# The gates' activation by tanh, one projection at a time and written over the projection's sum, in a fused attention and gating kernel

## The chip, the cores and the metric

The kernel runs on one core of a Trainium2 chip. The metric is the device time of one execution in microseconds; the median of several runs counts. Before the change it is 807.99 us (three runs: 807.52, 807.99 and 809.23).

Five engines work side by side, each through its own queue of instructions in order: TensorE (PE) multiplies matrices into the accumulators of PSUM, VectorE (DVE) and ScalarE (ACT) work on elements, GpSimd (POOL) does a few selections and issues DMAs, SyncE (SP) issues most DMAs.

## The reference

One layer of a trunk on 512 tokens of width 2048: a norm, attention over a sliding window of 128 keys with 32 heads of 64 (4 heads of keys and values), a gate on the attention's output, an output projection, and a second gate that adds an embedding. Cut to what matters here:

```python
hn = rmsnorm(x, norm_g)
q, k, v, gate = split(hn @ w_in)                 # gate: 512 x 2048
...
out = einsum('bnhgqj,bnjhd->bnqhgd', probs, vb)  # attention, 512 x 2048
y = (out * jax.nn.silu(gate)) @ w_out            # silu(x) = x * sigmoid(x)
x = x + y
x = x + (p @ ple_proj) * sigmoid(rmsnorm(x, ple_norm) @ ple_gate)
return rmsnorm(x, final_g)
```

The change concerns `out * silu(gate)` alone.

## The kernel before

All large products are made of three matmuls each (lines 120 to 122): every operand is split into a high part `hi`, a rounded copy made by ACT, and a low part `lo`, the difference made by DVE. Weights come by DMA as raw tiles of 128 x 1024; ACT makes `whi` (line 106) and DVE `wlo` (line 107), in pools of three buffers, two tiles ahead of their use.

The work has four parts, one after another on PE.

1. The start: keys, values and the first two tiles of queries, out of the first part of the weights.
2. The attention stage, from about 73 to 461 us. Thirty projection units, fourteen of queries (`qps`) and sixteen of gates (`gps`, gate c = 0 to 15, a pair of heads each), of 48 matmuls of 128 x 512 each, are dealt out in small portions between 64 attention blocks. Block i gives the scores of four heads and 64 queries (line 376), which DVE and ACT turn into probabilities (lines 385 to 408: bias, maximum, exponential, sum, scaling). Two blocks later `turn` transposes them on PE (418) and splits the result into `r`: a copy by ACT (420) and a difference by DVE (421). In three blocks of four POOL then selects a part into `own` (430) and ACT copies a half of it (437). One block after that `weigh` multiplies with the values on PE (454, and 456 with `own`), and ACT and DVE gather the result into `U` (463, 464).
3. The output projection, seven products of half matrices per side (`ORDER_OUT`), whose left operands are forms of the gated values (sums and differences of quarters, line 651, split by 658, 659, 663 and 664) and whose weights come as pieces `braw`, split into `bhi` (558) and `blo` (559).
4. The second gate with its embedding, in the same manner, and the final norm and stores.

PE, SP and POOL take the attention stage's instructions in the order in which the code gives them. ACT and DVE are ordered by the scheduler, which places each instruction when its inputs are due; on the chip each engine then keeps to its order and waits where an input is late.

The gates: when the last matmul of a gate's unit is done, DVE multiplies the sum in PSUM with the norm's factor `rb` into one of the four tiles `gates[g]` of 128 x 4 x 512 (line 688), and this frees the PSUM bank (tag "p", two banks). When the four gates of a tile are there, `silu` runs one ACT instruction over the whole tile (line 483); for the last tile three gates together and then one. From then on the gates are open. As soon as also the values of their heads are weighed, `gate_value` multiplies gate and `U` on DVE (line 478), one gate at a time.

A function of ACT stands in a table that a load instruction brings in (ACT_TABLE_LOAD in the profile). The exponential of the attention and the Silu use different tables here, so the program has loads at lines 405 and 483.

Of the kernel before, what the change touches and what calls it, by code (L numbers as in the profile page):

```python
# [13 lines left out]
AF = mybir.ActivationFunctionType  # L14
ALU = mybir.AluOpType
# [38 lines left out]
def trunk_kernel(ctx: ExitStack, tc: tile.TileContext, a: dict):  # L54
    nc = tc.nc
# [22 lines left out]
    def quarter(name):  # L78
        return whole.tile([P, 4, S], F32, tag="quarter", name=name)

    def bank(name, tag):
        return others.get(tag, psum).tile([P, 512], F32, tag=tag, name=name)
# [34 lines left out]
    def mm3(ps, sh, sl, mh, ml, first, last, more=False):  # L117


        nc.tensor.matmul(ps, sh, mh, start=first, stop=False, skip_group_check=more)  # L120
        nc.tensor.matmul(ps, sh, ml, start=False, stop=False, skip_group_check=more)  # L121
        nc.tensor.matmul(ps, sl, mh, start=False, stop=last, skip_group_check=more)  # L122
# [47 lines left out]
    kinds, g = [], 0  # L170
# [11 lines left out]
    rb = kvq.tile([P, S], F32, name="rb")  # L182
# [3 lines left out]
    for k in range(KC):  # L186
# [13 lines left out]
        if k == 0:  # L200
# [3 lines left out]
            out=l, in0=xr, scalar=g1, in1=h.bitcast(F32), op0=ALU.mult, op1=ALU.subtract  # L204
# [15 lines left out]
        for t in range(2):  # L220
            c = slice(t * P, (t + 1) * P)
            mm3(kt_ps[t], wh[:, c], wl[:, c], h, l, f, e)
        for t in range(NB):
            c = slice(t * P, (t + 1) * P)
# [30 lines left out]
    def evac_q(c, ps):  # L255

        q = Q[c] = kvq.tile([P, UNITS, 2, HB], F32R, tag="q", name=f"q{c}", bufs=4)
        halves = slice(0, 64), slice(64, 128)
        for e in range(2):
            src = ps[halves[e]].rearrange("p (g q) -> p g q", q=HB)  # L260
            hi, lo = q[halves[e], :, e], q[halves[1 - e], :, e]
            nc.scalar.copy(hi, src)
            nc.vector.tensor_sub(lo, src, hi.bitcast(F32))
# [58 lines left out]
    U, T, PT, O, gates, biases = {}, {}, {}, {}, {}, {}  # L322
# [148 lines left out]
    weighed, open_gates, due = set(), set(), []  # L471
    ah, al = {}, {}

    def gate_value():

        c = due.pop(0)
        src = gates[c // 4][:, c % 4, :]
        nc.vector.tensor_mul(src, src, U[c // 2][:, c % 2])

    def silu(g, some):  # L480

        part = gates[g][:, some]
        nc.scalar.activation(part, part, AF.Silu)
        for c in range(4 * g + some.start, 4 * g + some.stop):
            open_gates.add(c)
            if c in weighed:
                due.append(c)

# [20 lines left out]
    def block(nm, r, c, jj, m):  # L511
        return a[nm][2 * (c - 1) + jj, 4 * (r - 1) + m]
# [158 lines left out]
    def projections():  # L671
        for m, (kind, c) in enumerate(kinds):
            ps = bank(f"{kind}ps{c}", "p")
            for k in range(KC):
                if m == len(kinds) - 1 and k % 8 == 0:
                    B.ahead(k // 8 - 2)
                if m == len(kinds) - 1 and 2 <= k:
                    next(first_form, None)
                wh, wl = W.get(2 * m + k // 8)
                mm3(ps, wh[:, k % 8, :], wl[:, k % 8, :], xh[k], xl[k], k == 0, k == KC - 1)  # L680
                if k == KC - 1:
                    if kind == "q":
                        evac_q(c, ps)
                    else:
                        g = c // 4
                        if c % 4 == 0:
                            gates[g] = quarter(f"gate{g}")
                        nc.vector.tensor_mul(gates[g][:, c % 4, :], ps, rb)
                        if g == 3 and c % 4 >= 2:
                            silu(g, slice(0, 3) if c % 4 == 2 else slice(3, 4))  # L690
                        elif c % 4 == 3:
                            silu(g, slice(0, 4))
                yield

    proj = projections()

    during = ExitStack()
# [9 lines left out]
    for i in range(blocks + 3):  # L707

        if 2 <= i < blocks + 2:
            turn(i - 2)  # L710
        if 3 <= i:
            weigh(i - 3)
        if i < blocks:
            scores(i)
            first_chores(i)
            if i in (6, 20, 36):
                make_key(1 + i // 16)
        todo = left // (blocks + 2 - i) if i < blocks + 2 else 0
        left -= todo
        for n in range(todo):  # L720
            if n == 5 and due:
                gate_value()
            next(proj)
        if i < blocks:
            for n in range(i * SUM_STEPS // blocks, (i + 1) * SUM_STEPS // blocks):
                sum_weights(n)
    for _ in proj:
        pass
    while due:
        gate_value()  # L730
# [32 lines left out]
    def unit(p, jj, at, forms, todo):  # L763

        ps = banks(p, jj, forms.nm)
        f = forms.made[p]
        first = p not in (6, 5, 3)
        for m in range(4):
            bh, bl = B.get(at[p, jj] + m)
            for kk in range(2):  # L770
                k = 2 * m + kk
                fh, fl = f[m]
                for tb in range(2):
                    mm3(ps[tb], fh[:, kk, blk(tb)], fl[:, kk, blk(tb)], bh[kk], bl[kk], first and k == 0, k == 7, not first)
            some_later(4 - m)
            todo()
        return ps
# [52 lines left out]
    for n, p in enumerate(ORDER_OUT):  # L830
        nxt = out_forms.steps(ORDER_OUT[n + 1]) if n < 6 else iter(())
        for jj in range(2):
# [15 lines left out]
            ps = unit(p, jj, at_out, out_forms, todo)  # L848
# [101 lines left out]
    for n, p in enumerate(ORDER_PLE[:-1]):  # L950
        nxt = ple_forms.steps(ORDER_PLE[n + 1])
        for jj in range(2):
# [16 lines left out]
            ps = unit(p, jj, at_ple, ple_forms, todo)  # L969
# [51 lines left out]
    g = block(0, 0, "s", "o")()  # L1021
# [10 lines left out]
    g = block(1, 0, "s", "t")()  # L1032
# [10 lines left out]
    g = block(0, 1, "p", "o")()  # L1043
# [12 lines left out]
    g = block(1, 1, "p", "t", slice(0, 256))()  # L1056
# [74 lines left out]
```

## Time and profile before

| what | before |
|---|---|
| median of three runs | 807.99 us |
| the profiled execution, its own time | 807.1 us |
| its span in the profile | 805.1 us |
| ACT, table loads at lines 405 and 483 | 8 x 1.283 us |
| ACT, Silu (line 483) | 3 x 1.916, 1.492 and 0.631 us |
| DVE, gate times `rb` (line 688) | 16 x 0.686 us |
| DVE, gate times value (line 478) | 16 x 0.682 us |

A line of the timeline gives the start in us from the span's start, the duration, the engine, the line of the kernel, the operation, what it writes and reads, and in brackets the idle time of the engine before it and what ended this. A line of the groups gives the count, the busy time in us and the mean ns of one, then the idle time before them. A line of the waits gives who waited for whom: us in total, times, the longest.

### The profile page before, as it was taken

The numbers are of one execution on the slowest core, as the hardware profiler recorded it, in microseconds if no ns is written. First come the engines' busy times: TensorE is split into PE (matmuls) and PEld (weight loads), VectorE is DVE, ScalarE is ACT, GpSimd is POOL, SyncE is SP. The second block draws the span as 40 slices with busy tenths as digits, with TensorE's granted clock in tenths as the row PEclk, the third lists the DMA queues.
The fourth block names the chain that finished last, engine by engine and source line by source line (L and its number), as shares of the span: only waits on it lengthen the run. The fifth ranks groups of instructions, "written<-read, shape, count | busy, mean of one in ns | idle before, by whom it ended". The sixth has DMA issues, their size and how long they took to land.

```text
span 805.1 us, 11083 instructions
## 1 busy us (share of the span) xinstructions
PE 792.3 (98%) x3828; PEld 664.8 (83%) x3828; DVE 583.4 (72%) x951; ACT 508.4 (63%) x1034; POOL 111.1 (14%) x216
## 2 busy tenths in 40 slices
PE   9999999999999999999999999999999999999995
PEld 8888888878888888888888888888888888878884
DVE  4547676777767787776777898766646977889685
ACT  5644466676667786666586754555568856758545
POOL 0102113122121313122121100030000020210000
PEclk9999999999999999999999999999999999999998
DMA  8762687768697877877685469898512996895533
GB/s 330 288 196 89 170 277 196 222 186 212 163 255 216 192 235 187 219 184 220 180 211 142 118 215 359 326 283 240 198 53 85 368 204 208 168 212 193 183 105 105
DMA packets 45144, 164.91 MB, mean 205 GB/s; under 512 B 5904, under 2 KB 8080, under 8 KB 41248
## 3 DMA queue, kind: packets, MB, share of 16 engines
q1 hardware_dynamic: 38080, 130.07, 47.5%
q0 software_dynamic: 6720, 33.61, 22.6%
q8 instruction: 30, 0.49, 0.2%
q10 hardware_dynamic: 288, 0.52, 0.2%
q14 instruction: 26, 0.21, 0.1%
HBM read 158.36 MB, written 46.19 MB: 254 GB/s over the span
## 4 chain that ended last, share of the span: by engine, by line
PE 86%; issue 8%; DVE 2%; POOL 1%; DMA 1%; ACT 0%; ACTq 0%; POOLq 0%; DVEq 0%
PE qps L122 7%; PE qps L121 7%; PE qps L120 7%; PE gps L121 7%; PE gps L122 7%; PE gps L120 7%; PE o L122 6%; PE o L121 6%; PE o L120 6%; PE s L376 2%; PE g L121 2%; PE g L122 2%; PE g L120 2%; PE o L454 2%; PE pt L418 2%
## 5 line engine op out<-in xcount | busy, mean ns | idle before, releaser
L559 DVE TENSOR_TENSOR blo<-braw,bhi 128x1024 fp32r<-128x1024 f32 x80 | 97.8, 1222 | 39.9 <-ACT bhi L558 39.7
L558 ACT CAST bhi<-braw 128x1024 fp32r<-128x1024 f32 x80 | 84.0, 1050 | 56.9 <-PE o L122 17.5
L122 PE MATMUL gps<-xh,wlo 128*128 128x512 f32 x256 | 100.2, 391 | 0.0
L121 PE MATMUL gps<-xl,whi 128*128 128x512 f32 x256 | 100.2, 391 | 0.0
L120 PE MATMUL gps<-xh,whi 128*128 128x512 f32 x256 | 99.9, 390 | 0.0
L107 DVE TENSOR_TENSOR wlo<-wraw,whi 128x1024 fp32r<-128x1024 f32 x60 | 73.3, 1222 | 23.8 <-ACT whi L106 20.7
L122 PE MATMUL qps<-xh,wlo 128*128 128x512 f32 x224 | 87.8, 392 | 0.0
L121 PE MATMUL qps<-xl,whi 128*128 128x512 f32 x224 | 87.7, 391 | 0.0
L120 PE MATMUL o<-bhi,fho 128*128 128x512 f32 x224 | 87.7, 391 | 0.0
L122 PE MATMUL o<-bhi,flo 128*128 128x512 f32 x224 | 87.2, 389 | 0.0
L121 PE MATMUL o<-blo,fho 128*128 128x512 f32 x224 | 87.2, 389 | 0.0
L120 PE MATMUL qps<-xh,whi 128*128 128x512 f32 x224 | 87.2, 389 | 0.0
L106 ACT CAST whi<-wraw 128x1024 fp32r<-128x1024 f32 x60 | 62.9, 1049 | 27.9 <-PE gps L121 13.3
L405 ACT ACTIVATE t<-t,sm 128x129 f32<-128x129 f32 x128 | 50.6, 397 | 45.1 <-DVE sm L402 45.1
L121 PE MATMUL g<-blo,fhg 128*128 128x512 f32 x192 | 74.9, 390 | 0.4 <-DVE blo L559 0.4
L120 PE MATMUL g<-bhi,fhg 128*128 128x512 f32 x192 | 75.1, 391 | 0.0
L122 PE MATMUL g<-bhi,flg 128*128 128x512 f32 x192 | 74.8, 390 | 0.0
L430 POOL TENSOR_SCALAR_AFFINE_SELECT own<-r 64x512 fp32r<-64x512 f32 (+1 forms) x48 | 33.1, 690 | 298.4 <-DVE r L421 293.6
L122 PEld LDWEIGHTS gps<-xh,wlo 128*128 128x128 f32 x256 | 48.0, 188 | 10.2
L120 PEld LDWEIGHTS gps<-xh,whi 128*128 128x128 f32 x256 | 48.1, 188 | 9.0
L121 PEld LDWEIGHTS gps<-xl,whi 128*128 128x128 f32 x256 | 48.1, 188 | 8.9
L559 DVE TENSOR_TENSOR blo<-grown,bhi 128x1024 fp32r<-128x1024 f32 x32 | 39.1, 1222 | 17.4 <-ACT bhi L558 17.4
(202 smaller groups left out, 1725.2 us busy)
## 6 DMA issues: line engine op xcount, KB each, us to landing
wraw<-in_w_gate_in SPq DMA_DIRECT2D x32, 512.0 KB, 5.5
wraw<-in_w_q SPq DMA_DIRECT2D x28, 512.0 KB, 4.7
w_out<-in_w_out POOLq DMA_DIRECT2D x24, 512.0 KB, 7.6
braw<-in_w_out SPq DMA_DIRECT2D x24, 512.0 KB, 3.5
braw<-in_ple_gate SPq DMA_DIRECT2D x24, 512.0 KB, 3.4
w_out<-in_w_out SPq DMA_DIRECT2D x16, 512.0 KB, 6.1
ple_gate<-in_ple_gate SPq DMA_DIRECT2D x16, 512.0 KB, 5.7
ple_gate<-in_ple_gate POOLq DMA_DIRECT2D x16, 512.0 KB, 7.4
```

Source lines behind the costliest of these rows:

```text
L106: nc.scalar.copy(hi, raw)
L107: nc.vector.tensor_sub(lo, raw, hi.bitcast(F32))
L120: nc.tensor.matmul(ps, sh, mh, start=first, stop=False, skip_group_check=more)
L121: nc.tensor.matmul(ps, sh, ml, start=False, stop=False, skip_group_check=more)
L122: nc.tensor.matmul(ps, sl, mh, start=False, stop=last, skip_group_check=more)
L376: nc.tensor.matmul(s_ps[:, u, : 2 * n], st, key[:, :, first : first + n], start=True, stop=True)
L405: nc.scalar.activation(su, su, AF.Exp, bias=sm[:, u : u + 1], accum_out=sm[:, 2 + u : 3 + u])
L418: nc.tensor.transpose(pt[:, u * P : (u + 1) * P], pr[:, u, :], ident)
L430: nc.gpsimd.affine_select(out=flat(own), in_=flat(r).bitcast(F32), pattern=[[0, 8], [sign, HB]], compare_op=ALU.is_ge, fill=0.0, base=-HB ...
L454: nc.tensor.matmul(out, first, r[:, low], start=low == 0, stop=own is None and low == 1)
L558: nc.scalar.copy(hi, raw)
L559: nc.vector.tensor_sub(lo, raw, hi.bitcast(F32))
```

## The change

Each gate is opened by itself when its unit is done. With x the projection times `rb`, ACT writes tanh(x / 2) to PSUM over the unit's sum, and DVE makes (1 + tanh(x / 2)) * x, which is 2 * x * sigmoid(x), into the gate's tile. The missing half goes into the product with the values, which takes a scalar of 0.5. The calls of `silu` for a whole tile are gone.

```diff
         src = gates[c // 4][:, c % 4, :]
-        nc.vector.tensor_mul(src, src, U[c // 2][:, c % 2])
-
-    def silu(g, some):
-
-        part = gates[g][:, some]
-        nc.scalar.activation(part, part, AF.Silu)
-        for c in range(4 * g + some.start, 4 * g + some.stop):
-            open_gates.add(c)
-            if c in weighed:
-                due.append(c)
+        nc.vector.scalar_tensor_tensor(
+            out=src, in0=src, scalar=0.5, in1=U[c // 2][:, c % 2], op0=ALU.mult, op1=ALU.mult
+        )
+
+    def open_gate(c, ps):
+
+
+        x = gates[c // 4][:, c % 4, :]
+        nc.vector.tensor_mul(x, ps, rb)
+        nc.scalar.activation(ps, x, AF.Tanh, scale=0.5)
+        nc.vector.scalar_tensor_tensor(out=x, in0=ps, scalar=1.0, in1=x, op0=ALU.add, op1=ALU.mult)
+        open_gates.add(c)
+        if c in weighed:
+            due.append(c)
...
                         if c % 4 == 0:
                             gates[g] = quarter(f"gate{g}")
-                        nc.vector.tensor_mul(gates[g][:, c % 4, :], ps, rb)
-                        if g == 3 and c % 4 >= 2:
-                            silu(g, slice(0, 3) if c % 4 == 2 else slice(3, 4))
-                        elif c % 4 == 3:
-                            silu(g, slice(0, 4))
+                        open_gate(c, ps)
```

Lines behind line 483 stand four lines further down in the changed kernel (559 becomes 563, for instance) up to the gates' call, and as many as before behind it. The prediction names lines as the kernel before has them, except where it speaks of the new ones.

## The prediction

> **What bounds the kernel now.** I read the page first, then the busy time by stretches, the waits of TensorE, and the timeline around the longest of them.
>
> ```profile
> span 805.1 us, 11083 instructions
> PE 792.3 (98%) x3828; PEld 664.8 (83%) x3828; DVE 583.4 (72%) x951; ACT 508.4 (63%) x1034; POOL 111.1 (14%) x216
> ...
> 120.00:180.00 60.00, 59.55 (x292) 49.68 (x290) 43.18 (x87) 41.29 (x107) 11.95 (x24) 1.00 0.75 207
> 180.00:240.00 60.00, 58.65 (x286) 49.23 (x287) 43.60 (x91) 39.08 (x109) 14.04 (x30) 1.00 0.79 202
> 240.00:300.00 60.00, 60.00 (x294) 50.32 (x293) 46.76 (x95) 44.23 (x113) 12.57 (x26) 1.00 0.78 220
> 460.00:470.00 10.00, 10.00 (x48) 8.30 (x47) 9.86 (x15) 7.42 (x11) 0.00 (x0) 1.00 0.36 112
> ...
> PE o L456 <- ACT own L437: 1.5, 1, 1.5
> ...
> PE g L121 <- DVE blo L559: 0.4, 1, 0.4
> PE o L454 <- DVE r L421: 0.3, 1, 0.3
> ```
>
> In a stretch the columns are its length, then the busy time of PE, weight loads, DVE, ACT and POOL, the granted clock, the DMA share and GB/s. TensorE is the bound: 98% busy at a granted clock of 1.00 in these stretches, and the view of waits holds no others than these three and one at the warm-up. An edit on ACT and DVE can therefore give only what PE waits for them, and can take only by making PE wait anew. After the start, the waits are 1.5 + 0.3 us, both near 180 us (the 0.45 us and 1.35 us that PE misses in the two stretches around it are the same 1.8), and 0.4 us on a piece of weights in the last stage.
>
> The gates' Silu stands right before the 1.8 us:
>
> ```profile
> 173.06 0.38 PE L418 MATMUL pt<-ident,t 128*128 128x128 f32 x2
> 173.51 0.28 PE L456 MATMUL o<-own,DV 128*128 128x256 f32 x1
> 173.63 0.40 PE L376 MATMUL s<-k,q 128*128 128x256 f32 x2
> 174.44 0.69 ACT L408 ACTIVATE t<-t,sm 128x128 f32<-128x128 f32 x2
> 174.57 1.23 DVE L107 TENSOR_TENSOR wlo<-wraw,whi 128x1024 fp32r<-128x1024 f32 x1
> 175.15 1.28 ACT L483 ACT_TABLE_LOAD   x1
> 176.45 1.92 ACT L483 ACTIVATE gate<-gate 128x2048 f32<-128x2048 f32 x1
> 178.27 0.35 ACT L420 CAST r<-pt 128x256 fp32r<-128x256 f32 x1
> 178.67 0.38 PE L418 MATMUL pt<-ident,t 128*128 128x128 f32 x2
> 179.01 0.42 DVE L421 TENSOR_TENSOR r<-pt,r 128x256 fp32r<-128x256 f32 x1
> 179.49 1.37 POOL L430 TENSOR_SCALAR_AFFINE_SELECT own<-r 64x512 fp32r<-64x512 f32 x1 [8.86 <-DVE r L421]
> 180.90 0.40 ACT L437 CAST own<-own 64x256 fp32r<-64x256 f32 x1 [0.75 <-POOL own L430]
> 181.35 0.39 PE L456 MATMUL o<-own,DV 128*128 128x256 f32 x1 [1.49 <-ACT own L437]
> 181.58 0.40 PE L376 MATMUL s<-k,q 128*128 128x256 f32 x2
> ```
>
> The tile transposed at 173.06 is ready for ACT's copy (L420) at 173.44, but on ACT the table load and the Silu of four gates at once lie ahead of it: the copy starts at 178.27. Then the subtraction (L421), POOL's selection and the copy of `own` follow one another, and PE stands before L456 until 181.35. From the transposes to the scores PE takes 173.63 - 173.06 = 0.57 us in the block before and 181.58 - 178.67 = 2.91 us here. So this stall costs **2.34 us**: the two waits and the pipeline's refill.
>
> **The change part by part.** The rows that price it, and two later places that it touches:
>
> ```profile
> L385 DVE SCALAR_TENSOR_TENSOR t<-s,sclq,t 128x384 f32<-128x384 f32 x48 | 29.6, 617 | 1.2
> L688 DVE TENSOR_TENSOR gate<-gps,rb 128x512 f32<-128x512 f32 x16 | 11.0, 686 | 2.9 <-PE gps L122 2.8
> L478 DVE TENSOR_TENSOR gate<-gate,u 128x512 f32<-128x512 f32 x16 | 10.8, 682 | 5.4 <-ACT gate L483 5.4
> L385 DVE SCALAR_TENSOR_TENSOR t<-s,sclq,t 128x128 f32<-128x128 f32 x8 | 2.8, 344 | 0.1
> L651 DVE TENSOR_TENSOR gate<-gate 128x1024 f32<-128x1024 f32 x2 | 2.8, 1440 | 0.0
> L659 DVE SCALAR_TENSOR_TENSOR flo<-gate,fho 128x512 fp32r<-128x512 f32 x4 | 2.6, 684 | 0.0
> ...
> L405 ACT ACT_TABLE_LOAD x4 | 5.1, 1283 | 1.4 <-DVE sm L402 1.3
> L483 ACT ACT_TABLE_LOAD x4 | 5.1, 1283 | 0.1
> L882 ACT ACTIVATE z<-g,rstd 128x512 f32<-128x512 f32 x4 | 2.7, 686 | 1.9 <-PE g L122 1.9
> L917 ACT COPY s<-g 128x512 f32<-128x512 f32 x4 | 2.4, 593 | 0.7 <-PE g L122 0.7
> L483 ACT ACTIVATE gate<-gate 128x512 f32<-128x512 f32 x1 | 0.6, 631 | 0.0
> ...
> 268.08 1.23 DVE L107 TENSOR_TENSOR wlo<-wraw,whi 128x1024 fp32r<-128x1024 f32 x1 [0.40 <-ACT whi L106]
> 270.40 0.40 ACT L437 CAST own<-own 64x256 fp32r<-64x256 f32 x1
> 272.38 0.28 PE L456 MATMUL o<-own,DV 128*128 128x256 f32 x1
> ...
> 452.33 0.69 DVE L478 TENSOR_TENSOR gate<-gate,u 128x512 f32<-128x512 f32 x1 [1.51 <-ACT gate L483]
> 467.12 1.22 DVE L559 TENSOR_TENSOR blo<-braw,bhi 128x1024 fp32r<-128x1024 f32 x1
> 469.06 0.39 PE L121 MATMUL o<-blo,fho 128*128 128x512 f32 x1
> ```
>
> *Removed.* Five Silu calls and, by the instruction order of the changed kernel, seven of the eight table loads of this stage: one load is left, ahead of the first tanh, and the exponentials after it need none. 7 x 1.283 = 9.0 us leave ACT, and the Silu's own lengths are cut into pieces of 512.
>
> *Added on ACT.* Sixteen tanh over 128x512. The nearest row is the Silu of the same size, 0.631 us, which writes to SBUF. No row shows ACT writing PSUM; from below I bound it by the copy of that size, 0.593, from above by the sigmoid, 0.686, and take 0.63. Sixteen make 10.1 us, under the Silu's five calls plus their loads.
>
> *Added on DVE.* Sixteen products (1 + tanh) times x, 128x512, one operand from PSUM. Below stands L659, 0.684 (both from SBUF); above, L385's slope carried on: (617 - 344) / 256 = 1.07 ns per element, so 617 + 128 x 1.07 = 0.75 us. I take 0.69, by L688, which reads the same bank: 11.0 us in all. DVE has room for them over the stage (43 to 47 us busy in each of the 60 us stretches above).
>
> *Changed.* The product with the values gets a scalar 0.5: 0.684 (L659) instead of 0.682 (L478), nothing. The Trainium skill speaks against it: the page Vector Engine (DVE) Microarchitecture Reference, "Points that are easy to get wrong", has this form with two non-bf16 SBUF sources at half throughput. By that rule each would take about 1.2 us, 8 us more DVE in all, and the two at the hand-over below would cost PE about 0.5 us. The trace does not agree: 0.684 for just such sources.
>
> *At the stall.* In the new order ACT has the exponentials' scaling (ends 175.13), then tanh, then the copy L420; DVE has the weights' subtraction (ends 175.80), then the new product, then L421. So tanh ends at 175.13 + 0.63 = 175.76 and the copy L420 at 176.11; the product ends at 175.80 + 0.69 = 176.49 and L421 at 176.91. POOL's selection takes 1.37 at most, so 178.28, and the copy of `own` ends at 178.68. Without the stall PE wants it 0.45 us after the transposes (173.51 against 173.06 in the block before), at 179.12: 0.4 us to spare, more if POOL is faster. The stall goes whole: **-2.34 us**.
>
> *The same phase 91 us later.* There no Silu is in the way, so it shows the normal spare: the copy of `own` ends at 270.80 and PE takes it at 272.38, 1.58 us. The new product, queued between L107 (268.08) and L421, delays this by about 0.7: 0.9 is left, no stall. At most other gates the tanh is done before the next tile is transposed, so nothing that PE wants is behind it.
>
> *PSUM.* The projection's bank is now held until the new product has read it. With two banks it is wanted again one unit of 48 matmuls later, about 10 us (294 matmuls fill 60.00 us); the chain tanh and product is 1.3 us. Cost nothing; the cover is that unit.
>
> *The hand-over to the output projection.* From 460 to 470 us DVE is busy 9.86 of 10, and here cover is thin: the fourth piece of weights is ready at 467.12 + 1.22 = 468.34 for PE at 469.06, spare 0.72. Against the old order, up to that piece, DVE gets two new products (+1.38) and one subtraction of forms that moves forward (L651, +1.22, the length of any 128x1024 product such as L559); it loses two products with values that now come earlier, since their gates open singly (-1.36), and the wait of 1.51 at 452.33. I find one new wait of about 0.4 on the copies of the form. Sum +0.1: spare 0.6, no stall. Should it overrun, PE waits for the excess, which the later pieces do not add to.
>
> *Sum.* After this stage PE waits once, 0.4 us, for a piece of weights whose buffer PE's own progress frees, so I take all that follows to move along. The profiled execution took 807.1 us by its time (805.1 of span and 2.0 around it): 807.1 - 2.3 = 804.8. The median of the runs shown is 807.99, 0.9 above that execution, so I forecast 807.99 - 2.3 = **805.7 us**. Its own range is 805.0 to 806.4: from a fast set of runs to 0.7 us given back.
>
> **The rivals.** *(a) Part is given back at the hand-over.* For it: DVE at 9.86 of 10. Against it: the sum above leaves 0.6. The two form subtractions in its L651 row took 1.44 on average, not 1.22; with three of them so long before that piece (+0.66) and the new products at 0.75 (+0.12) DVE comes 0.9 later than before, 0.2 past its spare, and with two more waits like the one of 0.4 that I found, 1.0: 806.7.
>
> *(b) The stall only changes its reason.* L420 and L421 at 176 still have a tanh and a product ahead, and `own` has 0.4 us to spare with a slow POOL. If POOL or DVE's place in its queue costs 2 us more than I give it, PE waits as long as before: 808.0. That the loads do not go would end here as well; the order speaks against it, and by the Trainium skill, ScalarE: Activation LUTs, "Table sets", exp and tanh share a set, which the one load left agrees with.
>
> *(c) Slower: the tanh ahead of the transposed tile.* ACT takes tanh before L420 and DVE the product before L421 in four blocks (near 175, 268, 437 and 450 us). A tanh waits for DVE's first product, and the product for the tanh; L420 and L421, and PE behind them, wait for both. I give this chain 1.3 us; spare is 0.4 in the first and 0.9 in the second, and I count no more than 0.9 in the last two. If the hands from engine to engine make it come 2.5 us later than worked out, PE loses 2.1 + 3 x 1.6 = 6.9: 807.99 - 2.3 + 6.9 = 812.6. It decides against the change by more than noise from 1.75 us on (1.35 + 3 x 0.85 = 3.9, the gain of 2.3 and 1.6). Against it: DVE follows ACT promptly in the rows above (L421 at 179.01 after L420's 178.62, 0.39 us later), and the new product's neighbours are short.
>
> **How the numbers follow.** Forecast 64%, (a) 14%, (b) 8%, (c) 14%. Around 0.2%, 1.6 us, is what a measurement of this kernel can tell from no change; that line lies at 806.4. Of the forecast 62 are faster and 2 same; of (a) 3 faster and 11 same; of (b) 7 same and 1 slower; (c) is slower. So 65% faster, 20% same, 15% slower. The range from 804.9 to 808.2 holds nearly all of the forecast, (a) and (b) and leaves (c) out.
>
> **What would show it.** Right: no wait of L456 on `own` near 180 us, 0.57 us from transposes to scores there; one table load before the output projection; sixteen tanh of about 0.63 and sixteen products of about 0.69; `own` ready 0.4 to 1.2 us before PE in the blocks near 179 and 272; L559's fourth piece in the output projection about 0.6 us ahead of PE; PE's idle time after the start down to about 0.5 us. Wrong: a PE wait of over half a microsecond on L421, L437 or L559 where none stood before, a product over 0.8 us, or a stage of the same length in spite of the stall being gone.

## The result and the profile after

| what | before | changed |
|---|---|---|
| median, measured in turn on one chip | 808.61 us (6 runs, 807.52 to 809.73) | 805.53 us (6 runs, 805.19 to 805.97) |
| ratio of the medians, 95% interval | | 0.9965 [0.9954, 0.9976] |
| the profiled execution, its own time | 807.1 us | 805.41 us |
| its span | 805.1 us | 803.4 us |

The changed kernel is faster by 1.9 to 3.7 us, above the bound of 1.6. The two profiled executions are only 1.7 us apart; where the rest comes from is told below.

The busy time of the engines, from the page of the changed kernel, and then TensorE's waits after the start, from its view of waits (lines after the change have moved: L558 and L559 are now L562 and L563, L651 is L655, L659 is L663, L664 is L668; L686 to L688 became L486 to L488 inside `open_gate`):

```profile
span 803.4 us, 11106 instructions
PE 792.2 (99%) x3828; PEld 664.8 (83%) x3828; DVE 592.1 (74%) x967; ACT 501.1 (62%) x1038; POOL 111.9 (14%) x216
```

```profile
PE g L121 <- DVE blo L563: 0.5, 1, 0.5
PE o L456 <- ACT own L437: 0.3, 1, 0.3
```

PE's work is the same to 0.1 us, DVE has 8.7 us more and ACT 7.3 less. The waits of 1.5 and 0.3 us near 180 us are gone. The 0.5 is the known wait of the last stage, and the 0.3 is new: it stands at 401 us.

The view by stretches of the changed kernel, columns as in the prediction:

```profile
120.00:180.00 60.00, 60.00 (x298) 50.44 (x297) 45.93 (x94) 40.89 (x114) 13.09 (x27) 1.00 0.77 212
180.00:240.00 60.00, 60.00 (x292) 50.24 (x291) 45.60 (x94) 39.05 (x108) 12.88 (x26) 1.00 0.80 211
460.00:470.00 10.00, 10.00 (x45) 8.13 (x44) 9.94 (x14) 6.15 (x9) 0.00 (x0) 1.00 0.33 110
```

PE now fills both stretches around 180 us, where it missed 0.45 and 1.35. DVE is still full at the hand-over, 9.94 of 10.

The timeline of the changed kernel in the block of the former stall:

```profile
175.05 0.58 ACT L487 ACTIVATE gps<-gate 128x512 f32<-128x512 f32 x1
175.57 0.36 ACT L420 CAST r<-pt 128x256 fp32r<-128x256 f32 x1
175.72 0.68 DVE L488 SCALAR_TENSOR_TENSOR gate<-gps,gate 128x512 f32<-128x512 f32 x1
...
176.80 0.65 POOL L430 TENSOR_SCALAR_AFFINE_SELECT own<-r 64x512 fp32r<-64x512 f32 x1 [6.16 <-DVE r L421]
...
177.49 0.40 ACT L437 CAST own<-own 64x256 fp32r<-64x256 f32 x1
...
178.68 0.38 PE L418 MATMUL pt<-ident,t 128*128 128x128 f32 x2
...
179.13 0.28 PE L456 MATMUL o<-own,DV 128*128 128x256 f32 x1
...
179.25 0.40 PE L376 MATMUL s<-k,q 128*128 128x256 f32 x2
```

Before, ACT's copy L420 of the tile started at 178.27; now it starts at 175.57, since only one tanh stands ahead of it. `own` is ready at 177.49 + 0.40 = 177.89, and PE takes it at 179.13 with no wait in brackets: 1.24 us to spare. From the transposes to the scores it is 179.25 - 178.68 = 0.57 us, no longer 2.91.

The groups of the changed and added operations in the changed kernel:

```profile
L487 ACT ACT_TABLE_LOAD x1 | 1.3, 1283 | 0.0
L487 ACT ACTIVATE gps<-gate 128x512 f32<-128x512 f32 x16 | 9.5, 596 | 4.2 <-DVE gate L486 4.1
L488 DVE SCALAR_TENSOR_TENSOR gate<-gps,gate 128x512 f32<-128x512 f32 x16 | 10.9, 681 | 0.1
L478 DVE SCALAR_TENSOR_TENSOR gate<-gate,u 128x512 f32<-128x512 f32 x16 | 10.8, 682 | 0.1
```

One load is left of eight. The product with the half takes 682 ns, to the nanosecond what it took without. Two later places of the changed kernel, the block 91 us after the stall and the fourth piece of the output projection's weights with what comes ahead of it on ACT and DVE:

```profile
268.67 0.41 ACT L437 CAST own<-own 64x256 fp32r<-64x256 f32 x1
270.06 0.28 PE L456 MATMUL o<-own,DV 128*128 128x256 f32 x1
...
448.34 2.19 ACT L662 ACTIVATE fho<-gate 128x512 fp32r<-128x512 f32 x4
451.54 0.40 ACT L437 CAST own<-own 64x256 fp32r<-64x256 f32 x1 [1.01 <-POOL own L430]
451.97 0.36 ACT L463 COPY tmp<-o 64x256 f32<-64x256 f32 x1
452.37 0.43 DVE L464 TENSOR_TENSOR u<-o,tmp 64x256 f32<-64x256 f32 x1 [1.38 <-ACT tmp L463]
465.74 1.22 DVE L563 TENSOR_TENSOR blo<-braw,bhi 128x1024 fp32r<-128x1024 f32 x1
...
467.01 0.19 PEld L121 LDWEIGHTS o<-blo,fho 128*128 128x128 f32 x1 [0.23 <-DVE blo L563]
467.04 0.47 PE L121 MATMUL o<-blo,fho 128*128 128x512 f32 x1
```

In the first, 270.06 - 269.08 = 0.98 us are left of 1.58. At the hand-over the piece is ready at 465.74 + 1.22 = 466.96. PE's weight load for it (PEld) had to wait for the piece and starts at 467.01; in the kernel before, such a load starts 0.22 us ahead of its matmul (at 467.48 for the one at 467.70). The matmul itself starts at 467.04 and the next one at 467.35, 0.31 us later, where 0.23 is usual in this product. All four profiles of this order have 0.29 to 0.31 there. So nothing is left of the cover, and PE loses 0.08 us, too little for its view of waits to list it.

### The profile page after: what moved, and what is told of

Same layout as the page of the kernel before. It is cut to its first block, busy times and chain, and to the rows that moved or that the text cites. A ratio compares the mean times of both kernels' runs of the same rounds, so it can differ in the third digit from the quotient of the medians.

```text
span 803.4 us, 11106 instructions
## 1 busy us (share of the span) xinstructions
PE 792.2 (99%) x3828; PEld 664.8 (83%) x3828; DVE 592.1 (74%) x967; ACT 501.1 (62%) x1038; POOL 111.9 (14%) x216
## 4 chain that ended last, share of the span: by engine, by line
PE 96%; issue 1%; DVE 1%; ACT 1%; POOL 0%; ACTq 0%; DVEq 0%; POOLq 0%
PE gps L121 7%; PE gps L122 7%; PE gps L120 7%; PE qps L121 7%; PE qps L122 7%; PE qps L120 7%; PE o L120 6%; PE o L121 6%; PE o L122 6%; PE g L121 5%; PE g L122 5%; PE g L120 5%; PE s L376 2%; PE o L454 2%; PE pt L418 2%
## 5 line engine op out<-in xcount | busy, mean ns | idle before, releaser
L563 DVE TENSOR_TENSOR blo<-braw,bhi 128x1024 fp32r<-128x1024 f32 x80 | 97.8, 1222 | 43.6 <-ACT bhi L562 43.4
L562 ACT CAST bhi<-braw 128x1024 fp32r<-128x1024 f32 x80 | 84.1, 1051 | 61.9 <-DMA braw<-w_out 15.6
L563 DVE TENSOR_TENSOR blo<-grown,bhi 128x1024 fp32r<-128x1024 f32 x32 | 39.1, 1221 | 17.1 <-ACT bhi L562 17.1
```

The source lines that it names most:

```text
L562: nc.scalar.copy(hi, raw)
L563: nc.vector.tensor_sub(lo, raw, hi.bitcast(F32))
```

## The experiments

All times are medians; the ratio is to runs of the kernel before on the same chip in the same session, with its 95% interval.

**Both kernels once more.** No edit.

> The kernel before, once more. Theory (the change gains what TensorE waits for one block of the first gates' Silu): the profile shows the same 2.3 us from transposes to the end of the wait for own near 180 us, a span of 805 us, the same median as the runs beside it. The times of before so far lie in two groups, near 807.5 and near 809.6; rival (part of the measured 3.1 us is this spread and not the change): runs of both groups appear again, and the group near 809.6 has 2 us in places that the change does not touch.

> The changed kernel, once more. Theory: no wait for own near 180 us, span 803.4 us or a little less, ratio 0.9965 within 0.001. The new wait of 0.3 us for own near 401 us follows a pause of 0.35 us of VectorE ahead of a maximum (L402, near 393.6) that nothing in the profile ends: if it is a matter of the order it is there again, at the same place and length; if it is chance it is gone and the span is 0.35 us shorter.

Before: 808.38 us (807.21 to 809.60) against 807.56 for the same kernel beside it, 1.0008 [0.9999, 1.0017]. Changed: 805.13 us (804.87 to 806.01), 0.9970 [0.9960, 0.9980]. The second profile of the kernel before, with a span of 806.8 us, shows what the first, with 805.1, does not. Its stall near 180 is the same, but look at the granted clock (the third column from the right) in the stretches behind it:

```profile
181.00:183.00 2.00, 1.26 (x5) 1.17 (x6) 1.49 (x4) 1.69 (x2) 1.68 (x5) 0.76 0.00 0
183.00:185.00 2.00, 2.00 (x6) 1.52 (x6) 1.01 (x4) 1.95 (x8) 2.00 (x6) 0.50 1.03 197
185.00:187.00 2.00, 2.00 (x10) 1.60 (x8) 0.39 (x2) 2.00 (x8) 0.11 (x1) 0.88 1.03 197
```

For 2 us PE gets half the clock, and part of the time on either side: 6 matmuls in the stretch from 183 to 185, where the first profile has 11 at 1.00. With the clock at either 0.50 or 1.00, the three stretches add up to (0.24 x 2 + 0.50 x 2 + 0.12 x 2) / 0.5 = 3.4 us at half. The starts of seven pairs of neighbouring matmuls in it lie 427 ns apart in place of 227, so 7 x 0.2 = 1.4 us are lost, and two pairs at the ends lose 0.2 more. The span is 1.7 us longer: this 1.6, and 0.4 in the start less 0.3 in the last stage. Single executions differ in the start as well: if the starts of the same matmuls are laid side by side, the eleven profiles of this document lie up to 1.1 us apart already at 73 us, before the first gate is made at 84; the first profiles of the two kernels are only 0.01 apart there. All runs of the kernel before, in and beside these experiments, sorted by their mean granted clock:

| mean clock | runs before | median before | runs of the changed kernel here |
|---|---|---|---|
| 0.994 or less | 28 | 809.0 us | 0 |
| 0.995 | 5 | 808.6 us | 1 (804.9 us) |
| 0.996 or more | 40 | 807.5 us | 6 (median 805.3 us) |

3.4 us at half the clock are 1.7 us of clock in 807, or 0.002 of the mean, just the difference between the rows. So the kernel before has two times, and the changed one is 2.2 us below the one and 3.7 below the other; a median of it depends on how many runs of each it holds.

**Which gates matter.** Tanh for the first four gates alone, and for all others alone:

```
-                        nc.vector.tensor_mul(gates[g][:, c % 4, :], ps, rb)
+                        if c < 4:
+                            open_gate(c, ps)
+                            yield
+                            continue
+                        nc.vector.tensor_mul(gates[g][:, c % 4, :], ps, rb)
```

(in the second `c >= 4`; the other gates keep the Silu and a scalar of 1.0 in the product).

> Only the first four gates (tile 0) go by tanh one at a time, the other twelve by Silu as before; 2 of the 8 table loads go. Theory (one wait, behind the Silu of tile 0): the whole gain, span 802.8 us, ratio 0.9965 like the whole change, no wait near 180 us. Rival (what counts is the work taken from ScalarE, 9.0 us of table loads in all): two sevenths of it, 0.7 us, ratio 0.999.

> The reverse: tile 0 by Silu as before, the other twelve gates by tanh; 5 of the 8 table loads go. Theory: no gain, the wait near 180 us stays at 2.3 us, span 805.1 to 805.6 us, ratio 1.000. Rival (ScalarE's work): five sevenths, about 1.7 us, ratio 0.998.

The first four alone: 804.98 us (804.51 to 805.43), 0.9966 [0.9953, 0.9978], as much as the whole change. The other twelve alone: 807.81 us, 1.0003 [0.9993, 1.0013], nothing, though five table loads went. The waits of PE after the start, in the kernel with the first four and in the one with the twelve:

```profile
PE g L121 <- DVE blo L572: 0.3, 1, 0.3
```

```profile
PE o L456 <- ACT own L437: 1.5, 1, 1.5
...
PE o L454 <- DVE r L421: 0.3, 1, 0.3
```

The whole gain stands in one block. The new wait at 401 us is in neither. The hand-over's loss, 0.07 us by the spacing, is in the one with the twelve alone, which has the last gates by tanh.

**Table load or size of the piece.** Tanh in place of the Silu over whole tiles (no load, same length; the gates are then tanh(x) and not x * sigmoid(x)), and the Silu for each gate by itself (more loads, shorter pieces):

```
-        nc.scalar.activation(part, part, AF.Silu)
+        nc.scalar.activation(part, part, AF.Tanh)
```

```
-                        if g == 3 and c % 4 >= 2:
-                            silu(g, slice(0, 3) if c % 4 == 2 else slice(3, 4))
-                        elif c % 4 == 3:
-                            silu(g, slice(0, 4))
+                        silu(g, slice(c % 4, c % 4 + 1))
```

> The kernel before with tanh in place of Silu over the same whole tiles (tanh(x) stands for x * sigmoid(x), so the gates' values are others): the seven table loads go, the length of the instruction of tile 0 stays 1.92 us. Theory (what lies ahead of the transposed tile's copy on ScalarE is late by its sum): the copy L420 starts at 175.15 + 1.92 = 177.07 instead of 178.27, and of the 2.34 us near 180 some 0.2 to 1.0 are left, by POOL's time; span 803.0 to 803.8 us. Rival (the loads alone do it): all 2.34 us gone, span 802.7. Rival (the length alone does it): nothing gained, 805.1.

> The kernel before with Silu one gate at a time, so 16 instructions of 512 instead of five: the length goes, the table loads rise from 8 to 31. Theory: ahead of the copy near 177 us stand one load and 0.63 us, 1.91 in all, as much as in the run with tanh over whole tiles, so 0.2 to 1.0 us of that wait are left; but each of the other gates now puts 1.3 to 3.2 us before what stands behind it on ScalarE, where the spare in the tightest blocks is 0.8 to 1.6 us, so some of these get a wait of up to 2 us: span between 804 and 809 us. Rival (ScalarE's work): 23 more loads, 29.5 us, cost as they gained, 0.3 us for each of ScalarE's, some 8 us more: 813.

Whole tiles: 806.32 us, 0.9977 [0.9968, 0.9986]. Pieces: 806.29 us, 0.9975 [0.9966, 0.9984]. Either half of the change brings most of the gain. The span with whole tiles, 804.8 us, is above the 803.0 to 803.8 that were expected, though the stall left over is within its 0.2 to 1.0: against the first profile of the kernel before, this execution lost 1.1 us ahead of 73 us, where no gate is at work. The block in the kernel with whole tiles, on its timeline:

```profile
176.13 1.90 ACT L483 ACTIVATE gate<-gate 128x2048 f32<-128x2048 f32 x1
...
179.16 1.37 POOL L430 TENSOR_SCALAR_AFFINE_SELECT own<-r 64x512 fp32r<-64x512 f32 x1 [7.43 <-DVE r L421]
...
181.02 0.39 PE L456 MATMUL o<-own,DV 128*128 128x256 f32 x1 [0.64 <-ACT own L437]
```

and in the kernel with pieces, first the groups of its table loads, then its timeline:

```profile
L483 ACT ACT_TABLE_LOAD x15 | 19.2, 1283 | 0.3
L405 ACT ACT_TABLE_LOAD x14 | 18.0, 1283 | 0.2
```

```profile
176.16 1.28 ACT L483 ACT_TABLE_LOAD   x1
177.46 0.63 ACT L483 ACTIVATE gate<-gate 128x512 f32<-128x512 f32 x1
...
179.56 0.40 ACT L437 CAST own<-own 64x256 fp32r<-64x256 f32 x1
...
180.13 0.28 PE L456 MATMUL o<-own,DV 128*128 128x256 f32 x1
...
271.17 0.19 PEld L456 LDWEIGHTS o<-own,DV 128*128 128x128 f32 x1 [0.18 <-ACT own L437]
```

Ahead of L420, ACT had 1.28 + 1.92 = 3.20 us of work before, 1.90 with whole tiles, 1.28 + 0.63 = 1.91 with pieces, and 0.58 after the change. PE loses 2.34, 0.80, nothing (0.17 us to spare) and nothing (1.24) in this block. That the second and the third differ at the same work of ACT comes mostly from POOL, whose selection took 1.37 us in the one and, between 178.88 and 179.53, 0.65 in the other. And 29 loads, 37.2 us of ACT, cost PE only 0.25 us in the attention stage, by the spacing of matmuls: in one block near 271 us, where a load and a Silu stand ahead of L420, it has to wait for `own`. ACT's sum of work is no price, and the rival that charged it fell. That the pieces still are about 1 us above the changed kernel agrees with this 0.25 and with a loss of 0.71 on a piece of weights at 484.87 us, in the output projection; whether this second loss is there in every execution, one profile does not show.

**Twice the new work.** The first product and the tanh are issued twice, with the same result:

```
         nc.vector.tensor_mul(x, ps, rb)
+        nc.vector.tensor_mul(x, ps, rb)
         nc.scalar.activation(ps, x, AF.Tanh, scale=0.5)
+        nc.scalar.activation(ps, x, AF.Tanh, scale=0.5)
```

> The changed kernel with the first product (times rb) and the tanh of every gate done twice, the second time over the same place: 0.6 us more on ScalarE and 0.68 more on VectorE per gate, 9.5 and 10.9 us in all. Theory: in the attention stage the spare of own (0.99 us near 270, 1.24 near 179) takes it and TensorE waits nowhere anew by more than 0.3 us; at the hand-over, where the fourth piece of weights has 0.09 us to spare, two gates more bring 1.36 us and TensorE waits for about 1.2 us: span 804.6 to 805.2 us, ratio to before 0.999. Rival (the work itself costs): 3 us or more, spread over the stage, span over 806.

805.32 us (805.22 to 805.70), 0.9966 [0.9954, 0.9979]: 16 products of 0.69 and 16 tanh of 0.59 more cost nothing that can be measured. The wait at the hand-over that was expected did not come, for a reason that the timeline of DVE there shows:

```profile
464.31 1.22 DVE L565 TENSOR_TENSOR blo<-braw,bhi 128x1024 fp32r<-128x1024 f32 x1
465.56 0.69 DVE L490 SCALAR_TENSOR_TENSOR gate<-gps,gate 128x512 f32<-128x512 f32 x1
```

The scheduler chose another order: the fourth piece is split (L565) ahead of the new product, not behind it, and ends at 464.31 + 1.22 = 465.53, 1.87 us before PE starts on it at 467.40. A price per instruction cannot be read from this run; an order of DVE's queue can.

**A stall without Silu or loads.** To see whether the half clock is the stall's doing, the changed kernel gets a stall made by POOL alone: in that one block it makes the same selection six or eleven times.

```
+            for _ in range(6 if i == 14 else 1):
                 nc.gpsimd.affine_select(
...
```

> The changed kernel with one edit: in the block near 177 us (i = 14, the one where the kernel before stalled) POOL's selection into own is issued six times, with the same input, place and result; everywhere else once. No ScalarE or VectorE instruction is added. One selection took 0.65 us here and own had 1.24 us to spare, so PE should wait 5 x 0.65 - 1.24 = 2.0 us for own and lose some 2.5 us with the pipeline's refill, about the 2.34 us of the kernel before. Theory (it is TensorE's own wait that costs, and in part of the runs a granted clock of 0.50 for some matmuls follows such a wait, whatever caused it): the runs fall into two groups as those of the kernel before do, about 807.6 us at a mean clock of 0.996 or 0.997 and about 809 us at 0.993 or 0.994; 807.0 to 809.5 as a median. Rival (the low clock in part of the runs of the kernel before comes from the Silu and its table loads, or from the chip alone): all runs at 0.995 to 0.997 as the changed kernel's, about 807.6 us.

> As the one before it, with eleven selections in that block: PE should wait 10 x 0.65 - 1.24 = 5.3 us and lose some 5.8 us. Theory: the longer the wait, the more of the runs are followed by the low clock; at 5.3 us nearly all, so the times lie near 805.1 + 5.8 = 810.9 plus 1.4 to 2, about 812.5 us, with mean clocks of 0.994 or less. Rival (the wait does not lower the clock): 810.9 us at 0.995 to 0.997 in all runs.

Six: 809.79 us (808.12 to 812.22, 11 runs), 1.0020 [1.0009, 1.0030]. Three runs at a mean clock of 0.997 took 808.1 to 808.8 us, eight at 0.994 or 0.995 took 809.6 to 812.2. Eleven: 814.54 us (814.19 to 816.23, 5 runs), 1.0080 [1.0066, 1.0094], all at 0.991 or 0.992. Timeline of the one with six, then its stretches:

```profile
177.08 4.26 POOL L431 TENSOR_SCALAR_AFFINE_SELECT own<-r 64x512 fp32r<-64x512 f32 x6 [6.17 <-DVE r L421]
...
181.83 0.39 PE L457 MATMUL o<-own,DV 128*128 128x256 f32 x1 [2.28 <-ACT own L438]
```

```profile
182.00:184.00 2.00, 2.00 (x9) 1.62 (x10) 1.43 (x5) 1.90 (x6) 2.00 (x7) 0.72 0.50 66
184.00:186.00 2.00, 2.00 (x6) 1.57 (x5) 1.29 (x3) 1.90 (x8) 0.92 (x3) 0.50 1.12 217
186.00:188.00 2.00, 2.00 (x9) 1.63 (x8) 0.15 (x1) 0.70 (x2) 0.00 (x0) 0.92 0.96 172
```

and stretches of the one with eleven, where PE waited 5.87 us until 186.07:

```profile
184.00:186.00 2.00, 0.00 (x0) 0.00 (x0) 0.12 (x1) 0.39 (x1) 1.86 (x6) 0.72 0.00 0
186.00:188.00 2.00, 1.93 (x6) 1.74 (x7) 1.19 (x4) 1.20 (x6) 2.00 (x7) 0.50 0.45 66
188.00:190.00 2.00, 2.00 (x6) 1.52 (x6) 0.61 (x3) 1.95 (x5) 1.16 (x4) 0.50 1.03 197
190.00:192.00 2.00, 2.00 (x7) 1.57 (x6) 1.23 (x2) 1.39 (x6) 0.00 (x0) 0.57 1.10 180
```

The same sum as above gives (0.56 + 1.00 + 0.16) / 0.5 = 3.4 us at half clock after the wait of 2.28, and (0.56 + 1.00 + 1.00 + 0.86) / 0.5 = 6.8 us with the wait of 5.87, of which the first 1.2 lie in the wait itself. The theory holds: a wait of PE, with no Silu and no load near it, brings the half clock in part of the runs. Stalls of 0.8 us (whole tiles): none of 11 runs at 0.994 or less; 2.3 us: 28 of 73 (before) and 2 of 12 (the twelve gates alone); 2.4 us with six: 8 of 11 runs longer by some 1.4 us; about 6 us: all five. The share rises with the stall over these rows, but 2.3 and 2.4 us differ too little for their shares to be put down to length; what decides there is open. The price was too low: 814.5 and not 812.5, since a selection took 0.71 us and not 0.65, and the half clock lasted twice as long.

A version with tanh in a buffer of SBUF, to price the bank of PSUM, was not tried, so what writing to PSUM is worth by itself is open. The first four gates alone are level with the changed kernel, 804.98 and 805.13 us, closer than these runs can tell apart.

## Why the prediction was right, and where its sizes were off

**The stall** went whole, as *At the stall* has it, by the path that it names. `own` is ready at 177.89, where the sum allowed 178.68 at the latest: POOL took 0.65 us and not its limit of 1.37, and tanh 0.58. The two experiments with a part of the gates put the whole gain there.

**The durations.** *Added on ACT*: tanh 0.596 against 0.63, at the lower bound: what it was nearest to was ACT's other operation that touches PSUM (0.593), not the Silu of its own size. *Added on DVE*: 0.681 against 0.69. *Changed*: 0.682, as the row of L659 said and against the halved throughput of the Trainium skill, Vector Engine (DVE) Microarchitecture Reference, "Points that are easy to get wrong".

**The same phase 91 us later** has 0.98 us to spare, 0.9 was predicted; **PSUM** caused no wait of PE.

**The hand-over** is the step that was mis-sized: no cover is left where 0.6 us was predicted, and PE loses 0.08. Part of this is the starting figure: the 0.72 was read up to the matmul, but its weight load is due 0.22 earlier, so 0.50 was there. The rest is DVE, which comes 0.64 later against PE than before, and not 0.1. The wait found there as about 0.4 us is 1.38: on ACT four copies of the form (2.19 us) now run ahead of L437, this then waits 1.01 for POOL, the copy L463 stands behind it, and DVE's L464 behind that. Reordering gave about half of it back. Rival (a) thus came true, but by 0.08 us and not by 1.0.

**The sum** held for the median (805.7, measured 805.53 and 805.13), but 2.3 us is not what the pair of profiled executions shows. There the spans differ by 1.7, and the last matmul starts 1.6 us earlier: by the spacing of matmuls, the stall's 2.34, less 0.35 for the new wait at 401 us, 0.08 at the hand-over and 0.31 for longer waits on pieces of weights in the last stage. The last stage's waits differ from one execution to the next. The wait at 401 does not: in all four profiles of the changed order (two here, and those with six and eleven selections) L456 starts 0.58 to 0.60 us after the matmul ahead of it, where 0.12 is usual and the kernel before had 0.23. In the changed kernel it comes about so:

```profile
393.59 0.42 DVE L402 TENSOR_REDUCE sm<-t 128x2 f32<-128x258 f32 x1 [0.46 <-DVE t L400]
...
400.75 0.40 ACT L437 CAST own<-own 64x256 fp32r<-64x256 f32 x1 [2.81 <-POOL own L430]
...
401.20 0.39 PE L456 MATMUL o<-own,DV 128*128 128x256 f32 x1 [0.30 <-ACT own L437]
```

DVE pauses 0.46 us ahead of a maximum, and the chain from there to `own`, which was 0.11 us late already in the kernel before, comes later still. No releaser that the profile shows explains the pause, and it is left open. The prediction took all that follows this stage to move along and looked for thin cover only near the gates; a chain this thin, away from them, costs PE at once.

What brought the median back is that *Sum* carried the 0.9 us between profiled execution and median as if it belonged to every kernel. Part of it was the half clock after the stall, in four runs of ten, and it went with the stall: by an estimate from the table of clocks, 0.4 x 1.5 = 0.6 us on average. The changed kernel's median is only 0.1 above its profiled execution. So two errors of some 0.6 us have cancelled: that the forecast came within 0.2 us of the first median is partly luck.

**The rivals.** (b) fell: no wait near 180, one load. (c) fell: PE waits nowhere behind an L420 or L421 that has a new tanh or product ahead, and with every tanh and first product done twice nothing is lost in this stage. Of the list of what would show it, PE's idle time after the start is 0.8 and not 0.5 us, and the fourth piece is late instead of 0.6 us early; the rest came as written.

## What to carry to other kernels

Price a change on a helper engine by the few instructions that stand ahead of what the bound engine needs next, not by the engine's sum: 29 table loads in one stage cost 0.25 us there, one block's queue cost 2.3 us. Where a stall of the bound engine goes, ask whether some runs pay for it twice, by a lower clock behind it; a spread in the times of the kernel before is the hint. And list the spares of all chains that come round with the same period, as those with a few tenths left decide what a new order costs.

## What the runs showed of the hardware

In these runs PE's granted clock fell to 0.50 after stalls of 2.3 and 2.4 us in part of the runs, for 3.4 us in the two profiles that show it, and with the stall of about 6 us in all five by their mean clock, for 6.8 us in the one profiled. The page TensorE: Matmul & The Clock Gate of the Trainium skill, "Part 1: The HAM clock gate", has two states, 427 ns between cold matmuls of 512 columns and a free-running window of about 3.4 us; the trace agrees with the states, with its 427 ns and with stretches of 3.4 and twice 3.4 us. It asks for a whole idle window before the clock falls, which the wait of 2.28 us is not; how much of a window has to be idle, these runs do not show.

POOL's selection over 64x512 took 0.65 us in the changed kernel, and in the kernel before 1.37, from 179.49 to 180.86, with a product of DVE beside it that reads two operands from SBUF:

```profile
179.67 0.67 DVE L478 TENSOR_TENSOR gate<-gate,u 128x512 f32<-128x512 f32 x1
```

The selection is longer by 0.72 us, about the length of that product, as if it had stood still for so long. The Trainium skill, GPSIMD Engine Reference, "8. Key points", has them share their interface to SBUF when DVE reads two inputs from it; these two rows agree. The difference makes 0.72 of the 0.84 us by which the spare at the stall, 1.24 us, is over the 0.4 of the prediction.
